# An opening rearranged: an early table request, row factors one product ahead, and copies and sine arguments moved from VectorE to ScalarE

## The chip, the cores and the metric

The kernel runs on one core of a Trainium2 chip. A core has five engines that run side by side, each in the order of its own list of instructions: TensorE (PE in the profile; its weight loads are shown apart as PEld), VectorE (DVE), ScalarE (ACT), GpSimd (POOL) and SyncE (SP). Instructions of one engine wait for those of another, and for data transfers (DMA), by semaphores. Transfers are issued here almost all by SP, a few by ACT. The metric is the device time of one execution in microseconds (us), as the median of several runs.

## The reference

The kernel computes one layer of a bidirectional encoder on 2048 positions of 1024 channels (fp32). Cut to what the opening touches, and with the rest named in a line each, the reference does this:

```
u = rms_norm(h)                      # row factor rsqrt(mean(h*h) + eps), then a gain per channel
P = u @ W_in                         # one combined projection, columns partitioned
# Hyena group: width-3 convolution of v, x1, x2, then z <- x1 * (h1 * z + d1 z); z <- x2 * (h2 * z + d2 z)
#   the filters h1, h2 come from a small sine network over position features:
hid  = sin(fr1 * (feat @ w1 + b1))
hid  = sin(fr2 * (hid @ w2 + b2))
filt = (hid @ w3) * decay window;    spectrum = rfft(filt)
# mLSTM group: width-3 convolution, chunkwise scan in both directions, output gate
# group norms, output projection, residual; cross-attention into mem, residual; squared-ReLU MLP, residual; final norm
```

What matters is that the row factor of the norm is one number per position, so that the projection can be made of the unscaled rows (times the gain) and multiplied by the row factor afterwards; and that the argument of each sine is a sum and a product, `fr * (v + b)`, which is the same as `fr * v + b * fr`.

## The kernel before, in words

Every fp32 matmul is made of three in a reduced type: an operand is split into a high part (a cast by ACT, L365) and a low part (the difference, by DVE, L365), and `mm3` issues high by high (L354), low by high (L357) and high by low (L358). A *product* of the input projection is 128 output columns by 512 positions: eight slices k of the channels, three matmuls each, 24 in all, into one of four banks of the accumulator called `mm`. A second set of four banks, `hy`, takes the small matmuls.

The projection's method `sweep` makes the products in order and counts them in `self.made`. Positions come in chunks of 512. For the first chunks, `x_first` loads the transposed rows x (tiles `xt`, and `a` for the second chunk), makes the operands `xh` (ACT, L557) and `xl` (DVE, L558), squares them on ACT (L563), adds the squares up on DVE (L565), sums over the channels with four one-column matmuls (`columns`, L570), takes the inverse root (L459 and the lines of `rsqrt`), spreads the result on a diagonal `dg` (DVE, L493), and makes of it with one matmul and an ACT copy the tile `rowb` of row factors (`rows`, L579 and L580). The drains of the products, `leave`, multiply each product by `rowb` on the way out of its bank (DVE, L752). They are held back in a list: up to three finished products may wait in their banks while a fourth is made.

Where these steps are placed among the matmuls is given by a table of hooks, keyed by (products made, slice k):

```
self.hooks = {(0, 5): second, (1, 5): lambda: operands(range(4)), (2, 1): lambda: columns(0), (2, 2): halfway,
              (3, 1): lambda: rows(0), (5, 1): lambda: columns(1), (5, 6): lambda: rows(1), (6, 0): third}
```

The written order is not the final one. A scheduler orders each engine's instructions by its own estimate of times; `keep_in_program_order` (pinning) holds an instruction at its written place against that, and `behind` holds a matmul only behind the matmul that was written before it. In the kernel before, the first of the four one-column matmuls and the matmul of `rows` are held by `behind`.

Into the projection is woven `filters`, which makes the Hyena filters: a matmul of the features (L275), a sine, a second matmul (L278), a sine, and from the hidden layer the filter blocks in groups (matmuls L177, L190; DVE L330 to L335; POOL L336; an ACT copy L314 and a store). One sine over 128 by 512 is six DVE instructions and the ACT function: `u = (v + b) * fr` (L250), the nearest multiple of two pi (L253, L254), its subtraction in two steps (L257, L258), a clamp (L259), and Sin on ACT (L260). There are eight sines. Behind a product, when its convolution is done (ACT L762, DVE L764, L765), `sweep_out` transposes it on PE (L791), and the helper `copy` brings the transposed tiles from the bank to a staging tile `st`, turn by turn on ACT (L205) and on DVE (L207), whence SP stores them.

Later chunks are loaded by `x_chunk` (loads L518 on SP, row factors L503, product with gain and factor on DVE L507, splits L365). Far behind the opening, the mLSTM scan (L1215 to L1320) is interleaved by the scheduler with the output projection, which belongs to another part of the program and has no line of the change in it.

Of the kernel before, what the change touches and what calls it, by code (L numbers as in the profile page):

```python
# [133 lines left out]
class Prog:  # L134
    def __init__(self, ctx, tc, a):
        self.tc, self.nc, self.a = tc, tc.nc, a
        nc = self.nc
        self.ctx = ctx
        self.dr = ctx.enter_context(tc.tile_pool(name="dr", bufs=1, space=DRAM))
        self.s = {}  # L140
        cp = self.cp = ctx.enter_context(tc.tile_pool(name="cp", bufs=1))
        ident = cp.tile([128, 128], F32, name="ident")
        nc.gpsimd.memset(ident, 1.0)
        nc.gpsimd.affine_select(ident, ident, pattern=[[-1, 128]], compare_op=ALU.is_equal, fill=0.0,
                                base=0, channel_multiplier=1)
        self.ident = ident
        self.eps = cp.tile([128, 1], F32, name="eps")
        nc.vector.memset(self.eps, EPS)
        self.ones = cp.tile([128, 128], F32, name="ones")
        nc.vector.memset(self.ones, 1.0)  # L150
        self.flip = 0
        self.banks = []
        self.pending = []
        self.prepq = None
        self.hooks, self.made, self.lag, self.rowb = {}, 0, [], None
        self.rbp = cp.tile([128, 16], F32, name="rbp")
        cp.tile([128, 8], F32, name="even")
        par = self.par = cp.tile([128, 192], F32, name="par")
        nc.scalar.dma_start(out=par, in_=a["par"])
        self.g_mix, self.g_mem, self.gx, self.gf = (par[:, 8 * i:8 * i + 8] for i in range(4))  # L160
        self.cw = par[:, 32:92].rearrange("p (i c) -> p i c", i=3)
        self.cb, self.gb = par[:, 92:112], par[:, 112:128]
        self.ps = ctx.enter_context(tc.tile_pool(name="ps", bufs=1, space=PSUM))
# [37 lines left out]

    def copy(self, out, in_):
        self.flip ^= 1
        if self.flip:
            self.nc.scalar.copy(out, in_)  # L205
        else:
            self.nc.vector.tensor_copy(out, in_)  # L207
# [28 lines left out]
    def filters(self):  # L236
# [3 lines left out]
        if True:  # L240
            fw = sb.tile([128, 1280], F32, name="fw")
            nc.sync.dma_start(out=fw, in_=a["fw"])
            w1, w2, w3 = fw[0:66, 0:128], fw[:, 128:256], fw[:, 256:1280].rearrange("p (o c) -> p o c", o=2)
            par = self.par[:, 128:132]
            f1 = sb.tile([128, 128], F32, name="f1")
            nc.sync.dma_start(out=f1, in_=a["c_f1"])

            def sine(dst, src, b, fr, first=False):
                u, k = tb(), tb()
                d = nc.vector.tensor_scalar(u, src, par[:, b:b + 1], par[:, fr:fr + 1], ALU.add, ALU.mult)  # L250
                if first:
                    tc.keep_in_program_order(d)
                nc.vector.tensor_scalar(k, u, 1.0 / TWO_PI, MAGIC, ALU.mult, ALU.add)  # L253
                nc.vector.tensor_scalar(k, k, -MAGIC, None, ALU.add)  # L254
                c1 = 6.28125
                c2 = TWO_PI - c1
                nc.vector.scalar_tensor_tensor(u, k, -c1, u, ALU.mult, ALU.add)  # L257
                nc.vector.scalar_tensor_tensor(u, k, -c2, u, ALU.mult, ALU.add)  # L258
                nc.vector.tensor_scalar(u, u, -PI_F, PI_F, ALU.max, ALU.min)  # L259
                nc.scalar.activation(dst, u if len(dst.shape) == 2 else u.rearrange("p (m g j) -> p m g j", g=2, j=16), AF.Sin)  # L260
# [270 lines left out]
    def x_first(self):  # L531
# [35 lines left out]
        def columns(c):  # L567
            p = self.hy()
            for t in range(4):
                d = nc.tensor.matmul(p[:, t:t + 1], ssum[c][:, 128 * t:128 * t + 128], self.ones[:, 0:1], start=True, stop=True)  # L570
                if t == 0:
                    self.behind(d)
            rx = self.rx[:, 4 * c:4 * c + 4]
            self.inv_rms(rx, p[:, 0:4])
            self.dg = self.diagonal(rx)

        def rows(c):
            p = self.hy()
            self.behind(nc.tensor.matmul(p, self.ones, self.dg, start=True, stop=True))  # L579
            nc.scalar.copy(self.rowb[c], p)  # L580
# [18 lines left out]
        def operands(ks):  # L599
            for k in ks:  # L600
                operand(x1, 1, k)
# [5 lines left out]
        def third():  # L607
            w2 = self.weights(sb, *self.items[2], kc=2, nbufs=4)
            self.wst = self.stream(sb, self.items[3:], w2, kc=2, nbufs=4)

        self.hooks = {(0, 5): second, (1, 5): lambda: operands(range(4)), (2, 1): lambda: columns(0), (2, 2): halfway,
                      (3, 1): lambda: rows(0), (5, 1): lambda: columns(1), (5, 6): lambda: rows(1), (6, 0): third}
        for _ in range(9):
            yield
        for c in (2, 3):
# [98 lines left out]
    def sweep(self, cols, hf, first, after=None):  # L714
# [3 lines left out]
        for run in [cols[:2]] + [[c2] for c2 in cols[2:]] if self.made == 0 else [[c2] for c2 in cols]:  # L718
# [7 lines left out]
            for c, c2 in [(c, c2) for c in range(2) for c2 in run]:  # L726
                wh, wl = ws[c2]
                for m in range(2):
# [5 lines left out]
                    for k in range(8):  # L734
                        if (self.made, k) in self.hooks:
                            self.hooks.pop((self.made, k))()
                        self.mm3(p, wh[:, k, ms], wl[:, k, ms], xh[:, k, cs], xl[:, k, cs], k == 0, k == 7,
                                 k == 0 and 3 < self.made < 13)

                    def leave(c=c, m=m, c2=c2, p=p, cc=cc, Ps=Ps, run=run):  # L740
                        if c == 0:
# [1362 lines left out]
```

## Time and profile before

| | us |
|---|---|
| three runs | 3126.70, 3130.87, 3132.18 |
| their median | 3130.87 |
| the profiled execution's own time | 3127.22 |
| its span, first to last instruction | 3125.4 |
| PE busy in the span | 3031.2 (97%) |
| DVE busy | 1960.3 (63%) |
| ACT busy | 1487.1 (48%) |
| POOL busy | 1146.5 (37%) |

The profile is that of one execution. Its rows give an engine, a source line, an operation, the tiles written and read, the busy time, and in brackets the idle time of the engine ahead of it with what released it. A matmul that runs behind another overlaps its tail, so the distance between two starts says more than the printed length. The column PEclk of a stretch is the clock granted to TensorE as a share of full speed; its mean over the run is 0.987. The time between the span and the execution's own time is 1.8 us.

### The profile page before, as it was taken

The page shows a single profiled execution, that of the slowest core. Times are in us where ns is not written, and L with a number is a line of the kernel's source. Part 1 is how long each engine was busy: PE and PEld are TensorE (multiplying, and loading weights), DVE is VectorE, ACT ScalarE, POOL GpSimd, SP SyncE. Part 2 cuts the span into 40 slices and gives each one's busy share as a digit, 9 for nine tenths or more (in the row PEclk, how much of TensorE's full clock was granted, in tenths as well). Part 3 has the DMA queues.
Part 4 walks back from the last instruction along what each step waited for, and adds up shares of the span by engine and source line. Part 5 has one row for each costly group of instructions (what it writes and reads, how often), then busy time and mean ns, then how long its engine had stood idle before and what let it go on. Part 6 is the DMA issues. An engine that isn't in the chain of part 4 may idle for free.

```text
span 3125.4 us, 42916 instructions
## 1 busy us (share of the span) xinstructions
PE 3031.2 (97%) x14257; PEld 2377.4 (76%) x14257; DVE 1960.3 (63%) x3448; ACT 1487.1 (48%) x2907; POOL 1146.5 (37%) x802
## 2 busy tenths in 40 slices
PE   8999999989999898999999999999999999999998
PEld 6655667766677666888888888888888888888876
DVE  7965466446646455777765556557555686565695
ACT  5443366533656225555544455556555443333335
POOL 0122012200113343324141327776565475242693
PEclk9999999999999998999999999999999999999999
DMA  6564767676877897455385647656644565353524
GB/s 211 153 212 163 235 204 220 192 217 217 240 207 246 267 315 242 142 184 197 115 280 175 226 154 246 207 187 219 213 151 150 167 216 187 111 165 112 161 91 172
DMA packets 444101, 607.07 MB, mean 194 GB/s; under 512 B 38494, under 2 KB 248542, under 8 KB 442856
## 3 DMA queue, kind: packets, MB, share of 16 engines
q1 hardware_dynamic: 405988, 546.54, 54.5%
q10 hardware_dynamic: 37892, 57.79, 5.4%
q8 instruction: 113, 1.85, 0.2%
q14 instruction: 108, 0.88, 0.1%
HBM read 401.79 MB, written 202.41 MB: 193 GB/s over the span
## 4 chain that ended last, share of the span: by engine, by line
PE 84%; DMA 6%; DVE 4%; ACT 2%; issue 2%; POOL 1%; SPq 0%; ACTq 0%; DVEq 0%; POOLq 0%
PE mm L354 17%; PE mm L358 17%; PE mm L357 17%; PE hy L358 6%; PE hy L354 6%; PE hy L357 6%; PE hy L177 3%; PE mm L912 2%; PE hy L943 2%; PE hy L985 1%; DMA a<-hy 1%; PE hy L1279 1%; PE mm L674 1%; PE mm L703 1%; PE hy L1281 1%
## 5 line engine op out<-in xcount | busy, mean ns | idle before, releaser
L1623 DVE TENSOR_TENSOR bl<-wr,bh 128x512 fp32r<-128x512 f32 x213 | 240.3, 1134 | 129.9 <-ACT bh L1622 129.7
L1622 ACT CAST ah<-w 128x512 fp32r<-128x512 f32 x284 | 176.6, 623 | 301.5 <-PE hy L357 155.2
L365 DVE TENSOR_TENSOR wl<-wn,wh 128x512 fp32r<-128x512 f32 (+1 forms) x300 | 218.1, 773 | 99.9 <-ACT wh L365 99.4
L354 PE MATMUL mm<-xh,wh 128*128 128x512 f32 x640 | 267.5, 419 | 12.1 <-ACT wh L365 9.1
L990 POOL TENSOR_TENSOR b<-b,a 128x512 f32<-128x512 f32 x64 | 87.4, 1367 | 509.3 <-ACT b L988 214.5
L357 PE MATMUL mm<-xl,wh 128*128 128x512 f32 x640 | 255.6, 399 | 0.7 <-DVE xl L365 0.6
L358 PE MATMUL mm<-xh,wl 128*128 128x512 f32 x640 | 254.8, 399 | 0.0
L1622 ACT CAST bh<-wr 128x512 fp32r<-128x512 f32 x232 | 143.5, 621 | 229.1 <-PE mm L358 177.0
L1623 DVE TENSOR_TENSOR al<-w,ah 128x512 fp32r<-128x512 f32 x236 | 216.7, 918 | 55.4 <-ACT ah L1622 55.2
L358 PE MATMUL mm<-bh,al 128*128 128x512 f32 x576 | 224.0, 391 | 2.6 <-POOL al L1623 2.6
L354 PE MATMUL mm<-bh,ah 128*128 128x512 f32 x576 | 225.9, 392 | 0.4 <-DVE acc L1785 0.3
L357 PE MATMUL mm<-bl,ah 128*128 128x512 f32 x576 | 224.9, 390 | 0.0
L365 ACT CAST wh<-wn 128x512 fp32r<-128x512 f32 (+1 forms) x300 | 166.6, 618 | 113.8 <-PE mm L358 51.4
L357 PE MATMUL mm<-act,wh 128*128 128x512 f32 x512 | 200.5, 393 | 0.8 <-DVE act L365 0.8
L354 PE MATMUL mm<-act,wh 128*128 128x512 f32 x512 | 198.8, 394 | 2.5 <-ACT wh L365 2.4
L358 PE MATMUL mm<-act,wl 128*128 128x512 f32 x512 | 199.1, 392 | 0.0
L354 PE MATMUL hy<-bh,ah 128*128 128x512 f32 x448 | 175.2, 391 | 0.0
L357 PE MATMUL hy<-bl,ah 128*128 128x512 f32 x448 | 174.6, 390 | 0.0
L358 PE MATMUL hy<-bh,al 128*128 128x512 f32 x448 | 174.4, 390 | 0.0
L354 PEld LDWEIGHTS mm<-xh,wh 128*128 128x128 f32 x640 | 121.3, 190 | 67.2 <-issue 19.0
L354 PE MATMUL mm<-wh,xh 128*128 128x256 f32 (+1 forms) x512 | 155.9, 305 | 10.6 <-ACT xh L365 8.1
L336 POOL TENSOR_TENSOR b<-b 128x512 f32<-128x512 f32 x32 | 58.3, 1822 | 277.4 <-DVE b L333 137.6
(369 smaller groups left out, 8282.3 us busy)
## 6 DMA issues: line engine op xcount, KB each, us to landing
wr<-hc SPq DMA_DIRECT2D x224, 256.0 KB
w<-in_ff_w_dram SPq DMA_DIRECT2D x172, 256.0 KB
hc<-wn SPq DMA_DIRECT2D x128, 256.0 KB
wn<-in_w_in_dram SPq DMA_DIRECT2D x100, 256.0 KB
hc<-q SPq DMA_DIRECT2D x96, 256.0 KB
fs<-a SPq DMA_DIRECT2D x32, 512.0 KB
a<-fs SPq DMA_DIRECT2D x64, 256.0 KB
a<-zs SPq DMA_DIRECT2D x64, 256.0 KB
```

The lines of the kernel that those rows point to most:

```text
L177: b = self.nc.tensor.matmul(*products[-1], start=True, stop=True)
L336: nc.gpsimd.tensor_tensor(e[1], f, b, ALU.subtract)
L354: first = mm(ps, lh, rh, start=start, stop=False)
L357: mm(ps, lh, rl, start=False, stop=False)
L358: self.last = mm(ps, ll, rh, start=False, stop=stop)
L365: both = (self.nc.scalar.copy(hi, src), self.nc.vector.tensor_tensor(lo, src, hi.bitcast(F32), ALU.subtract))
L674: mul(p[:, m], w[:, k, ms], mt[k // 4][:, k % 4], start=k == 0, stop=k == 7)
L912: nc.tensor.matmul(pp, dm[:, m], t[:, m], start=True, stop=True)
L943: nc.tensor.matmul(pg, em[:, m], y, start=True, stop=True)
L990: nc.gpsimd.tensor_tensor(xt, xt, hi[:, m], ALU.mult)
L1622: self.nc.scalar.copy(hi, src)
L1623: eng.tensor_tensor(lo, src, hi.bitcast(F32), ALU.subtract)
```

## The change

Four things change. First, a small tile that held nothing becomes `fb`, and ACT's first instruction is a one-column copy of a constant into it, which needs no transfer; ACT's function table is thus asked for by that copy. Second, `copy` uses ACT for all of its copies as long as fewer than 28 products are made, in place of every other one; 14 copies change from DVE to ACT. Third, the argument of a sine is made on ACT as `fr * v + fb`, with `fb = b * fr` multiplied once on DVE for each of the two layers; the eight instructions of L250 leave DVE, and eight activations appear on ACT. The instruction pinned in a sine is now DVE's next one. Fourth, the hooks of the first chunk's `columns`, `halfway` and `rows` move from slices 1, 2 and 1 to slices 5, 6 and 5; the first one-column matmul of the first chunk is pinned in place of being held behind, and so is the first matmul of each slice with a hook in products 2 and 3.

```diff
-        cp.tile([128, 8], F32, name="even")
+        self.fb = cp.tile([128, 8], F32, name="fb")
+        nc.scalar.activation(self.fb[:, 4:5], self.eps, AF.Copy)
...
     def copy(self, out, in_):
         self.flip ^= 1
-        if self.flip:
+        if self.flip or self.made < 28:
             self.nc.scalar.copy(out, in_)
...
+            for i in (0, 2):
+                nc.vector.tensor_tensor(self.fb[:, i:i + 1], par[:, i:i + 1], par[:, i + 1:i + 2], ALU.mult)
...
                 u, k = tb(), tb()
-                d = nc.vector.tensor_scalar(u, src, par[:, b:b + 1], par[:, fr:fr + 1], ALU.add, ALU.mult)
+                nc.scalar.activation(u, src, AF.Identity, bias=self.fb[:, b:b + 1], scale=par[:, fr:fr + 1])
+                d = nc.vector.tensor_scalar(k, u, 1.0 / TWO_PI, MAGIC, ALU.mult, ALU.add)
                 if first:
                     tc.keep_in_program_order(d)
-                nc.vector.tensor_scalar(k, u, 1.0 / TWO_PI, MAGIC, ALU.mult, ALU.add)
...
-                if t == 0:
+                if t == 0 and c == 0:
+                    pin(d)
+                elif t == 0:
                     self.behind(d)
...
-        self.hooks = {(0, 5): second, (1, 5): lambda: operands(range(4)), (2, 1): lambda: columns(0), (2, 2): halfway,
-                      (3, 1): lambda: rows(0), (5, 1): lambda: columns(1), (5, 6): lambda: rows(1), (6, 0): third}
+        self.hooks = {(0, 5): second, (1, 5): lambda: operands(range(4)), (2, 5): lambda: columns(0), (2, 6): halfway,
+                      (3, 5): lambda: rows(0), (5, 1): lambda: columns(1), (5, 6): lambda: rows(1), (6, 0): third}
...
                         if (self.made, k) in self.hooks:
                             self.hooks.pop((self.made, k))()
+                            hook = True
+                        else:
+                            hook = False
                         self.mm3(p, wh[:, k, ms], wl[:, k, ms], xh[:, k, cs], xl[:, k, cs], k == 0, k == 7,
-                                 k == 0 and 3 < self.made < 13)
+                                 k == 0 and 3 < self.made < 13 or hook and self.made in (2, 3))
```

Lines below the first edit carry higher numbers in the changed kernel (L354 becomes L357, L570 becomes L573, L579 becomes L584, L752 becomes L760).

What the scheduler makes of it shows at three places. The first is PE at the end of the first four products: `hy` from `dg` and `ones` is the matmul of `rows`, `mm_328`, `mm_249` and `mm_329` are products, `mm_384` and `mm_387` the one after, and the matmul from `fw` is the filters' first. Between the one-column matmuls and the end of the four products, 18 matmuls stand in both programs. Before:

```order
L570 MATMUL hy_252<-ones_65,ssum0_98 128x1 x4
...
L354 MATMUL mm_328<-xh_87,wh_106 128x512
L357 MATMUL mm_328<-xl_88,wh_106 128x512
L358 MATMUL mm_328<-xh_87,wl_107 128x512
L579 MATMUL hy_332<-dg_272,ones_65 128x512
L275 MATMUL hy_370<-b_366,fw_361 128x512
L354 MATMUL mm_384<-xh_87,wh_104 128x512
```

And with the change:

```order
L573 MATMUL hy_265<-ones_65,ssum0_99 128x1 x4
...
L361 MATMUL mm_249<-xh_88,wl_108 128x512
L584 MATMUL hy_345<-dg_285,ones_65 128x512
L357 MATMUL mm_329<-xh_88,wh_107 128x512
...
L361 MATMUL mm_329<-xh_88,wl_108 128x512
L278 MATMUL hy_373<-b_369,fw_362 128x512
L357 MATMUL mm_387<-xh_88,wh_105 128x512
```

The one-column matmuls stay where they were; the matmul of `rows` now follows them by 9 matmuls in place of 18, and the other 9 follow it.

The second place is DVE at about 115 us of the span before, around the drain of a product of the second chunk and the third chunk's first operands (`xt`, `xl`); rows from `hy` and `a`, and `b` from `b`, are the filter blocks. Before:

```order
L207 COPY st<-mm 126x512
L233 SCALAR_TENSOR_TENSOR xr_y<-xr_t,xr_y 128x2
L460 COPY small<-xr_y 128x2
L752 TENSOR_TENSOR P<-mm,rowb_101 128x512
...
L764 SCALAR_TENSOR_TENSOR cv<-P,par,cv 128x1008
L507 SCALAR_TENSOR_TENSOR xt<-xt,par,rb 128x512 x4
L330 TENSOR_TENSOR b<-hy,a 128x512
L331 TENSOR_TENSOR b<-hy,a 128x512
L765 SCALAR_TENSOR_TENSOR cv<-P,par,cv 128x1008
L365 TENSOR_TENSOR xl<-xt,xh 128x2x512
```

With the change:

```order
L333 TENSOR_TENSOR b<-hy,a 128x512
L334 TENSOR_TENSOR b<-hy,a 128x512
L336 TENSOR_TENSOR b<-b 1x512
L338 TENSOR_TENSOR b<-b 128x512
...
L760 TENSOR_TENSOR P<-mm,rowb_102 128x512
...
L772 SCALAR_TENSOR_TENSOR cv<-P,par,cv 128x1008
L510 SCALAR_TENSOR_TENSOR xt<-xt,par,rb 128x512 x4
L773 SCALAR_TENSOR_TENSOR cv<-P,par,cv 128x1008
L333 TENSOR_TENSOR b<-hy,a 128x512
```

Two groups of filter blocks, seven DVE rows, now stand ahead of that drain; before, they stood between it and the rows of the next operands and behind them. On PE their matmuls stand some 25 matmuls earlier. The copy of `st` is gone from DVE here.

The third place is DVE at about 1257 us before, where the mLSTM scan (`rw`, `ht`) meets the output projection (`act`). Before:

```order
L365 TENSOR_TENSOR act<-hy,act 128x4x128
L220 SCALAR_TENSOR_TENSOR hy<-hy,bry 128x8
L1251 TENSOR_TENSOR rw<-rw,hy 128x512 x2
L1313 SCALAR_TENSOR_TENSOR ht<-ht,hy,gml 128x128 x8
L1448 TENSOR_TENSOR acc<-mm,acc 128x512
```

With the change:

```order
L368 TENSOR_TENSOR act<-hy,act 128x4x128
L1321 SCALAR_TENSOR_TENSOR ht<-ht,hy,gml 128x128 x8
L368 TENSOR_TENSOR act<-hy,act 128x4x128
L1259 TENSOR_TENSOR rw<-rw,hy 128x512 x2
L1240 STREAM_SHUFFLE rw<-rows_9565 128x512 x2
```

The two rows on `rw` now stand behind the eight on `ht` and a row of `act`, which they led. PE's counterpart is that the matmuls from `rw` (L1279, L1281) stand together behind four of the projection's. No line of the change is there; the order follows from the scheduler's estimate of all that lies ahead.

## The prediction, made before the result was known

> **What bounds the kernel now.** I read the page's shares first, then PE's waits in the first 300 us, then a table of stretches, then the timeline at each place that the change touches. The page and the table of waits:
>
> ```profile
> PE 3031.2 (97%) x14257; PEld 2377.4 (76%) x14257; DVE 1960.3 (63%) x3448; ACT 1487.1 (48%) x2907; POOL 1146.5 (37%) x802
> ...
> PE mm L354 <- ACT wh L365: 9.1, 1, 9.1
> PE hy L579 <- DVE dg L493: 3.0, 1, 3.0
> PE hy L190 <- DVE b L335: 1.1, 1, 1.1
> ...
> PE hy L177 <- issue: 0.2, 1, 0.2
> ```
>
> PE is busy for 97% of the span, so nothing that the change does to DVE or ACT counts unless PE waits for them. In the first 300 us PE waits in eleven rows only: 9.1 us for the first weights, 3.0 us for the diagonal of the row factors, and nine rows that add up to 6.5 us (only the first and last of these nine are shown). Stretches of that time show what PE got done:
>
> ```profile
> core 0: us, PE busy (x) PEld busy (x) DVE busy (x) ACT busy (x) POOL busy (x), PEclk, DMA share, GB/s
> 34.40:37.80 3.40, 0.42 (x1) 0.30 (x2) 2.61 (x13) 0.00 (x0) 0.00 (x0) 1.00 0.00 0
> 37.80:44.60 6.80, 6.80 (x14) 3.97 (x13) 4.75 (x8) 1.87 (x2) 0.00 (x0) 0.50 0.00 0
> 57.00:117.00 60.00, 59.05 (x276) 47.77 (x275) 54.03 (x132) 29.48 (x56) 0.00 (x0) 1.00 0.64 191
> 120.00:157.30 37.30, 31.79 (x133) 18.31 (x132) 37.29 (x58) 14.88 (x22) 8.15 (x4) 1.00 0.45 141
> 157.30:160.70 3.40, 3.40 (x14) 1.52 (x12) 2.10 (x4) 0.37 (x1) 1.75 (x1) 0.50 0.94 306
> 160.70:180.00 19.30, 19.22 (x86) 11.23 (x83) 14.11 (x21) 10.52 (x16) 4.48 (x2) 1.00 0.63 222
> 200.00:240.00 40.00, 40.00 (x193) 23.77 (x192) 21.98 (x33) 14.70 (x25) 10.96 (x7) 1.00 0.54 186
> ```
>
> The reader is to see three things. From 120 to 157.3 us DVE is busy for 37.29 of 37.30 us, ACT for 14.88, and PE makes 133 matmuls; at the rate of the undisturbed stretch (193 in 40 us) they would take 27.6. So DVE bounds that stretch, and 9.7 us are lost in it, more than the waits there that the profile names. Ahead of it, from 57 to 117 us, DVE is busy for 90% and PE hardly waits. And the granted clock is 0.50 in two stretches: for 6.8 us behind the wait for the diagonal, and for 3.4 us at the end of the DVE-bound stretch.
>
> **The change part by part.** *The early table request.* ACT's table load starts when the first x tile lands, because the first activation needs both:
>
> ```profile
> 5.87 1.28 ACT L557 ACT_TABLE_LOAD   x1 [5.87 <-DMA xt<-in_x_t_dram]
> 7.16 1.33 ACT L557 ACTIVATE xh<-xt,par 128x512 fp32r<-128x512 f32 x2
> 8.40 1.12 ACT L365 CAST wh<-a 128x512 fp32r<-128x512 f32 x2
> 9.06 0.80 PE L354 MATMUL mm<-xh,wh 128*128 128x512 f32 x1 [9.06 <-ACT wh L365]
> ...
> 29.14 0.95 PE L570 MATMUL hy<-ones,ssum 128*128 128x1 f32 x8
> 30.12 0.16 DVE L459 TENSOR_SCALAR ms<-hy 128x4 f32<-128x4 f32 x1 [0.98 <-PE hy L570]
> ```
>
> With the table loaded beforehand, the first activation starts at 5.87, 1.28 us sooner, and the casts and PE's start follow if the weights and the next x tiles are there. ACT worked without a gap from 7.16 to 9.06, which shows no tile missing then; whether all later ones lead by as much isn't shown. Bounds: +0.5 (the later tiles come when they come, and half of it is lost) to +1.28. I take +1.2, since ACT's rows show no wait there. The DVE chain behind the one-column matmuls moves along. The new copy of one column lies in time in which ACT only waits for a transfer: 0.
>
> *Row factors one product ahead.* The one-column matmuls stay in place among PE's rows, and so does the DVE chain between them and the diagonal (with the six or seven additions of the second chunk's squares in it). The matmul that uses the diagonal stands 9 matmuls nearer:
>
> ```profile
> 33.26 0.39 PE L358 MATMUL mm<-xh,wl 128*128 128x512 f32 x1
> 33.49 0.39 PE L354 MATMUL mm<-xh,wh 128*128 128x512 f32 x1
> ...
> 34.59 0.69 DVE L565 TENSOR_TENSOR ssum<-ssum,sq 128x512 f32<-128x512 f32 x1
> 36.45 0.87 DVE L493 TENSOR_SCALAR dg<-ident,small 128x128 f32<-128x128 f32 x4
> 37.38 1.69 PE L579 MATMUL hy<-dg,ones 128*128 128x512 f32 x2 [3.05 <-DVE dg L493]
> ...
> 39.72 2.48 DVE L752 TENSOR_TENSOR P<-mm,rowb 128x512 f32<-128x512 f32 x4 [2.40 <-ACT rowb L580]
> ```
>
> Two matmuls stand 0.23 us apart, so PE arrives 9 x 0.227 = 2.0 us sooner and waits 3.05 + 2.0 = 5.1 us instead of 3.05; the 9 matmuls are made afterwards. That is -2.0. The wait brings a clock drop of 6.8 us at 0.5 already, worth 3.4 us; a longer wait can bring one stretch of 3.4 us more (-1.7) or, since the idle stretch ends at another place of the clock's steps, one less (+1.7). Bounds -3.7 to -0.3, taken -2.0, the row with no change in the number of steps. For the drains at 39.72 nothing is won: they wait for the same diagonal. The pins alone move no row of PE beyond these.
>
> *Copies and sine arguments off DVE.* Their rows between 40 and 160 us:
>
> ```profile
> L250 DVE TENSOR_SCALAR b<-hy,par 128x512 f32<-128x512 f32 x8 | 6.4, 802 | 0.0
> L207 DVE COPY st<-mm 126x512 f32<-126x512 f32 x8 | 5.5, 681 | 2.6 <-DMA hy<-st 2.6
> L205 ACT COPY st<-mm 126x512 f32<-126x512 f32 x8 | 4.7, 583 | 6.4 <-PE mm L791 6.4
> ```
>
> DVE loses 6.4 + 5.5 = 11.9 us of work there, and the 2.6 us in which it waited for a store to free a staging tile; the other six of the 14 copies come later, where PE is full (19.22 of 19.30 us behind 160.7), and count nothing. ACT gains as much in rows of some 0.6 us in stretches where it is busy for 49% and 40%. How much reaches PE? In the DVE-bound stretch at most the 9.7 us of the count, with the low-clock stretch behind it 9.7 + 1.7 = 11.4; at least half of the nine named waits, 3.2. DVE's 11.9 us exceed the 9.7, so it should cease to be the bound; I take 10.0, near the count. Late next are ACT's casts of the third and fourth chunk's operands, which stand behind copies now:
>
> ```profile
> 138.88 0.73 PE L354 MATMUL mm<-xh,wh 128*128 128x512 f32 x2 [0.97 <-ACT xh L365]
> 152.75 1.05 ACT L365 CAST xh<-xt 128x1024 fp32r<-128x1024 f32 x1 [9.91 <-DVE xt L507]
> 154.33 0.51 PE L354 MATMUL mm<-xh,wh 128*128 128x512 f32 x1 [1.02 <-ACT st L205]
> ```
>
> The wait for such a cast costs 0.97 us now, and the second one has a slack of its own of 9.91 us on ACT, all DVE's; I let one such wait come back, -1.0. Net +9.0. The added wait: DVE now waits for ACT at the head of each sine, and behind it drains and splits are queued; L250 has 0.0 idle ahead of it in all eight, so its matmul was done long before DVE came, which leaves ACT time. The two one-column multiplications into `fb` take less than 0.2 us each (L459's row of 0.16 is the nearest) and lie before the first operands: 0. The compiled program asks for tables 12 times, as before, so the new Identity and Copy rows cost no table load.
>
> *The order at 1257 us.* The two rows on `rw`, for which PE's next four matmuls wait, go behind eight rows on `ht` and one on `act`:
>
> ```profile
> 1258.39 0.69 DVE L365 TENSOR_TENSOR act<-hy,act 128x512 fp32r<-128x512 f32 x1 [0.40 <-ACT act L365]
> 1259.55 1.28 DVE L1251 TENSOR_TENSOR rw<-rw,hy 128x512 f32<-128x512 f32 x2 [0.39 <-PE hy L1241]
> 1260.43 0.38 PE L1279 MATMUL hy<-va,rw 128*128 128x129 f32 x2
> 1260.76 2.22 DVE L1313 SCALAR_TENSOR_TENSOR ht<-ht,hy,gml 128x128 f32<-128x128 f32 x8
> ```
>
> They are 2.22 us later; four matmuls that PE makes meanwhile cover some 0.4. I take -1.8, with 0 (PE has more of the projection ready) and -3.5 (a low-clock stretch behind it, 1.7) as ends.
>
> **The sum.** +1.2 - 2.0 + 9.0 - 1.8 = +6.4 us: the profiled execution's 3127.2 becomes 3120.8. That execution lies 3.7 us under the median of the three runs; set off from the median, 3130.87 - 6.4 = 3124.5.
>
> One rule speaks against a part of this. The row: the second low-clock stretch, from 157.3, follows waits of 1.02, 0.46 and 0.64 us, none of them long. The Trainium skill, "TensorE: Matmul & The Clock Gate", section "Why this matters for your kernels", asks for no idle gap above about 3 us between bursts and says that one window of idleness drops the clock. With the first drop, behind 3.05 us, the trace agrees; the second came without such a gap, so the trace differs. By the rule it would have another cause than DVE's lateness and stay: 1.7 us less in the sum. I go by the rows, in which it ends a stretch that DVE bounds.
>
> A second one bears on the copies. The same copy takes 583 ns on ACT and 681 on DVE in the rows above. The Trainium skill, "ScalarE: Activation LUTs", section "Rules for kernel authors", would have adds and multiplies on VectorE rather than ScalarE. By it the eight sine arguments would stay, and the relief be 5.5 us instead of 11.9; the trace, where an ACT row of that size takes no longer than DVE's, doesn't bear it out.
>
> **The rivals.** (a) *Same: relief by the named waits only.* DVE's stretch is held in part by its own inputs, the x transfers of the later chunks, and the low clock at 157.3 stays:
>
> ```profile
> 143.67 4.08 SPq L518 DMA_DIRECT2D xt<-in_x_t_dram  x2
> 164.24 2.74 DVE L507 SCALAR_TENSOR_TENSOR xt<-xt,par,rb 128x512 f32<-128x512 f32 x4 [4.74 <-DMA xt<-in_x_t_dram]
> ```
>
> SP spends 4.08 us on two issues, and DVE waits 4.74 us for such a tile a little later. Against it: DVE has no idle time ahead of that in the stretch. Then the relief is half of 9.7 less the 1.0 that comes back, 3.9: 1.2 - 2.0 + 3.9 - 1.8 = +1.3, so 3129.6. The rule on the clock leads to nearly the same side: 6.4 - 1.7 = +4.7, 3126.2.
>
> (b) *Slower: ACT's queue.* All copies of that time stand on ACT, and a copy that waits for a store holds up every cast behind it. DVE paid 2.57 us for one such wait:
>
> ```profile
> 93.69 0.69 DVE L207 COPY st<-mm 126x512 f32<-126x512 f32 x1 [2.57 <-DMA hy<-st]
> ```
>
> Two such waits ahead of the first cast of each of the two chunks make 2 x 2 x 2.57 = 10.3 us, against which stands DVE's whole relief of 10.0; with the other terms it is 10.0 - 10.3 - 1.0 + 1.2 - 2.0 - 1.8 = -3.9, and with three at each chunk -9.0, 3139.9. It decides from the point at which casts are late by 13.7 us in all (3.7 beyond the relief, which with -2.6 of the other terms makes 6.3). Against it: ACT has some 52 us of idle time in the two stretches together, and only one copy of the sixteen waited.
>
> (c) *The early parts do nothing,* because x tiles and weights bound the start: 1.2 less, +5.2, 3125.7, which lies with (a).
>
> **How the numbers follow.** 0.2%, 6.3 us, is about what a measurement of this kernel can tell from no change. My sum lies just on it. Forecast, a gain of 6.3 us or more: 0.50. Within 6.3 us: 0.36, of it (a) 0.16, the clock's rule 0.10 and (c) 0.10. Slower by over 6.3 us, (b): 0.14. The lower end takes the best bounds, 1.28 - 0.3 + 11.4 = 12.4, from the fastest run, 3126.7 - 12.4 = 3114. The upper end: the worst of (a), 0.5 - 3.7 + 3.2 - 1.0 - 3.5 = -4.5, gives 3135.4; I round to 3135 and leave out (b) in its larger forms.
>
> **What the profile afterwards would show.** The first matmul at about 7.9 us, the load of the table before 5 us; the wait for the diagonal at 5 us, with a low-clock stretch of 6.8 us behind it; DVE below 90% in the stretch at 120 to 150 us and its 133 matmuls in about 28 us, no low clock behind it; a wait of PE for `rw` of about 2 us near 1250. I am wrong if the casts on ACT wait behind copies, if the named waits for `xh` and `xl` grow, or if transfers of x set the pace there.

## The result, and the profile after

| | before | changed |
|---|---|---|
| median, us | 3129.22 (3126.70 to 3132.18, 6 runs) | 3119.57 (3116.15 to 3121.71, 6 runs) |
| ratio | 1 | 0.9971, 95% interval 0.9961 to 0.9980 |
| profiled execution: own time, span | 3127.22, 3125.4 | 3121.71, 3120.0 |

The change makes the kernel 9.1 us faster by the ratio; 6.4 us were forecast, in a range that held the time. A later set of runs of the same two kernels (among the experiments below) gave 3125.36 against 3127.11, ratio 0.9990 (0.9981 to 0.9999), which is 3.1 us: the gain has the same sign both times, and its size is known no better than between these two. Over both sets, 17 runs of the changed kernel average 3121.6 and 35 of the kernel before 3127.4, a gap of 5.8 us.

The table of PE's waits in the first 300 us of the changed kernel, to be held against the eleven rows of before:

```profile
PE mm L357 <- ACT wh L368: 8.0, 1, 8.0
PE hy L584 <- DVE dg L496: 4.7, 1, 4.7
PE hy L191 <- DVE b L338: 1.3, 1, 1.3
PE mm L360 <- DVE xl L368: 1.3, 1, 1.3
PE hy L178 <- POOL b L339: 1.0, 1, 1.0
```

The first wait is 1.1 us shorter, the second 1.7 us longer, and of the nine others, 6.5 us together, three are left with 3.6 us. The stretches of the prediction, in the changed kernel (us, then busy time of PE, PEld, DVE, ACT and POOL with their counts, granted clock, DMA share, GB/s):

```profile
33.56:40.39 6.83, 4.37 (x8) 2.85 (x9) 3.77 (x14) 0.59 (x1) 0.00 (x0) 0.50 0.00 0
...
57.00:117.00 60.00, 60.00 (x280) 47.57 (x279) 50.77 (x125) 36.16 (x68) 3.19 (x2) 1.00 0.64 202
120.00:157.30 37.30, 35.03 (x163) 20.79 (x159) 34.32 (x54) 18.07 (x28) 6.89 (x4) 1.00 0.66 219
157.30:160.70 3.40, 2.06 (x8) 0.59 (x10) 2.49 (x4) 1.04 (x1) 0.00 (x0) 1.00 0.18 67
160.70:180.00 19.30, 19.23 (x88) 11.42 (x84) 18.01 (x23) 10.89 (x18) 4.99 (x3) 1.00 0.67 233
```

From 120 to 157.3 us PE makes 163 matmuls in place of 133, DVE is busy for 34.32 us in place of 37.29, and the low clock at the end of that stretch is gone. The start of the opening, and the wait for the diagonal:

```profile
1.29 1.28 ACT L158 ACT_TABLE_LOAD   x1 [1.29 <-PEq L2087]
...
5.95 1.33 ACT L560 ACTIVATE xh<-xt,par 128x512 fp32r<-128x512 f32 x2 [3.16 <-DMA xt<-in_x_t_dram]
7.33 1.14 ACT L368 CAST wh<-a 128x512 fp32r<-128x512 f32 x2
8.00 0.80 PE L357 MATMUL mm<-xh,wh 128*128 128x512 f32 x1 [8.00 <-ACT wh L368]
...
35.09 0.88 DVE L496 TENSOR_SCALAR dg<-ident,small 128x128 f32<-128x128 f32 x4
36.02 2.08 PE L584 MATMUL hy<-dg,ones 128*128 128x512 f32 x2 [4.68 <-DVE dg L496]
```

The table load lies at 1.29 us, where ACT has nothing else to do, and the first matmul comes at 8.00 in place of 9.06.

Waits alone don't show where the time went, so I counted PE's matmuls and took, for the Nth of them, how much earlier it starts in a kernel than in the trace of before. This is worked out from the traces, row by row; both traces have 14257 matmuls, and the few that change places within a stage blur a point by a microsecond or two, so that only points between stages are used.

```
Nth matmul                 80   140   320   450  1000  3000  4000  5200  6000 14256
its start before, us       29    49    90   119   246   648   872  1134  1309  3111
changed                   1.0   0.5   0.5   1.8   7.3   7.2   8.1   8.0   7.7   5.4
changed, second time      2.0   2.1   2.1   3.4   9.0   8.9   6.4   4.4   6.3   7.1
```

The table shows where time is won: 1 us at the start, a small loss or none at the row factors (between the 80th and the 140th), and 6.7 to 6.9 us between 90 and 246 us. Of the 2.0 us at the 80th matmul of the second trace, about 1 us is not the change's: the granted clock rises to full speed 2.9 us after the first matmul there, against 4.9 us in the trace of before and 5.1 us in the first trace of the changed kernel. From 246 to 648 us the lead stays to within 0.1 us. Behind 648 us the two executions of one program part by up to 3.6 us.

### The profile page after: what moved, and what is told of

It reads as the page before. It is cut to its first block, busy times and chain, and to the rows that moved or that the text cites. A ratio compares the mean times of both kernels' runs of the same rounds, so it can differ in the third digit from the quotient of the medians.

```text
span 3120.0 us, 42912 instructions
## 1 busy us (share of the span) xinstructions
PE 3025.7 (97%) x14257; PEld 2374.8 (76%) x14257; DVE 1957.9 (63%) x3428; ACT 1498.4 (48%) x2930; POOL 1145.9 (37%) x802
## 4 chain that ended last, share of the span: by engine, by line
PE 55%; DVE 2%; issue 1%; DMA 1%; ACT 0%; POOL 0%; SPq 0%; ACTq 0%; POOLq 0%; DVEq 0%
PE mm L357 12%; PE mm L360 12%; PE mm L361 12%; PE hy L361 6%; PE hy L357 6%; PE hy L360 6%; DVE bl L1631 1%; PE hy L1287 1%; PE hy L1289 1%; DVE acc L1923 0%; PE hy L1534 0%; DVE acc L1957 0%; PE hy L1423 0%; DMA e<-hg 0%; PE hy L1249 0%
## 5 line engine op out<-in xcount | busy, mean ns | idle before, releaser
L357 PE MATMUL mm<-xh,wh 128*128 128x512 f32 x640 | 267.5, 419 | 8.6 <-ACT wh L368 8.0
L357 PE MATMUL mm<-bh,ah 128*128 128x512 f32 x576 | 225.6, 392 | 0.1
L357 PE MATMUL mm<-act,wh 128*128 128x512 f32 x512 | 198.9, 394 | 1.4 <-ACT wh L368 1.3
L357 PE MATMUL hy<-bh,ah 128*128 128x512 f32 x448 | 175.2, 391 | 0.0
L357 PEld LDWEIGHTS mm<-xh,wh 128*128 128x128 f32 x640 | 121.2, 190 | 60.9 <-issue 18.6
L357 PE MATMUL mm<-wh,xh 128*128 128x256 f32 (+1 forms) x512 | 155.2, 304 | 12.6 <-ACT xh L368 10.2
L361 PEld LDWEIGHTS mm<-xh,wl 128*128 128x128 f32 x640 | 121.0, 189 | 47.9 <-issue 23.2
```

Source lines behind the costliest of these rows:

```text
L357: first = mm(ps, lh, rh, start=start, stop=False)
L361: self.last = mm(ps, ll, rh, start=False, stop=stop)
```

## The experiments

All are compared with the kernel before. The line numbers of each kernel differ a little, as its edits do.

**The early table request alone.**

```diff
-        cp.tile([128, 8], F32, name="even")
+        self.fb = cp.tile([128, 8], F32, name="fb")
+        nc.scalar.activation(self.fb[:, 4:5], self.eps, AF.Copy)
```

> The kernel before with the early table request alone. Theory: the first matmul starts at about 8.0 us in place of 9.06, and the 1.0 us is kept, since the one-column matmuls and the diagonal move along: 1.0 us faster at the end of the first 100 us, and about 1 us faster in all (3128), with 1.5 us either way from rows that the scheduler orders otherwise. Rival: the x tiles and weights take the 1.0 us back within the first four products, and nothing is left when the one-column matmuls start (29.1 us before).

Measured 3128.27, ratio 0.9995 (0.9985 to 1.0004). PE's lead is 1.1 us at the 80th and the 320th matmul, so it is not taken back in the opening. Of that 0.8 us is left at 246 us: PE's rows up to there stand in the order of before, and its wait for a sine near 97 us is 1.4 us in place of 1.0. Nothing is left at the end of its trace (-2.0). 1 us is below what the timed runs tell apart, and they show no difference. The theory holds in the trace only; the rival falls.

**The row factors' hooks and pins alone.**

```diff
-        self.hooks = {..., (2, 1): lambda: columns(0), (2, 2): halfway,
-                      (3, 1): lambda: rows(0), ...}
+        self.hooks = {..., (2, 5): lambda: columns(0), (2, 6): halfway,
+                      (3, 5): lambda: rows(0), ...}
...
-                if t == 0:
+                if t == 0 and c == 0:
+                    pin(d)
+                elif t == 0:
                     self.behind(d)
```

(with the pins of the matmuls at the hooks, as in the change).

> The kernel before with the row factors' hooks and pins alone. Theory: the wait for the diagonal grows from 3.05 to about 5 us, and between 0.4 and 2.0 us are lost there, more when the low clock falls on matmuls and less when it falls on the wait; nothing is won later: 3129.6 to 3131.2. Rival: drains that start 9 matmuls sooner spare PE waits for banks further on, and the kernel gets faster by 2 us or more (3127 or less).

Measured 3127.71, ratio 0.9995 (0.9985 to 1.0006). The wait is what the theory said:

```profile
PE hy L581 <- DVE dg L493: 5.1, 1, 5.1
```

but only 0.2 us are lost between the 80th and the 140th matmul, since the low clock lasts 3.4 us there and partly falls on the wait. At 246 us this kernel leads by 3.0 us: the order behind is another, and no low-clock stretch ends the DVE-bound stretch:

```profile
120.00:157.30 37.30, 33.49 (x152) 20.37 (x150) 37.29 (x60) 15.57 (x22) 8.97 (x5) 1.00 0.55 167
```

DVE is as full here as before (37.29 us), and PE makes 152 matmuls in place of 133. So a part of such a count, 2.6 us between the 320th and the 1000th matmul, can come without any work taken off DVE. Both theories miss: no loss, and no gain that the runs show.

**The change without the row factors' part,** measured twice (the second time beside the changed kernel).

```diff
-        self.hooks = {..., (2, 5): lambda: columns(0), (2, 6): halfway,
-                      (3, 5): lambda: rows(0), ...}
+        self.hooks = {..., (2, 1): lambda: columns(0), (2, 2): halfway,
+                      (3, 1): lambda: rows(0), ...}
```

(and without its pins).

> The changed kernel with the hooks and pins of before. Theory: the wait for the diagonal is back at about 3 us, and the kernel is 0.4 to 2.0 us faster than the changed one (3117.5 to 3119.2). Rival: the row factors' place carries part of the gain behind 120 us, and this is slower than the changed kernel by 2 us or more (3121.6 or more).

> The changed kernel with the hooks and pins of before, once more, beside the changed kernel on the same chip. Theory: 0 to 2 us faster than the changed kernel, since its trace is 1.2 us ahead at the 120th matmul. Rival: slower than it by 2 us or more.

> The changed kernel once more, as the measure for the other three on the same chip: 0.9961 to 0.9980 of the kernel before, as measured first.

Measured 3119.57, ratio 0.9970 (0.9959 to 0.9981), and 3120.05, 0.9979 (0.9970 to 0.9988); the changed kernel beside the second gave the 0.9990 (0.9981 to 0.9999) told above, which is outside what was expected of it. The wait is back at 2.6 us. PE's lead grows by 0.3 to 0.5 us between the 80th and the 140th matmul, where the changed kernel loses 0.5 or wins 0.1. So the row factors' place costs some 0.2 to 1.0 us, and carries little of the gain behind 90 us (between the 320th and the 1000th matmul 6.2 and 6.3 us are won without it, 6.7 and 6.9 with it). That is small enough that one pair of medians (3119.57 and 3119.57) shows none of it; the other pair, 5.3 us apart where 0 to 2 were expected, shows more than the traces account for.

**Copies and sine arguments together, and each alone.**

```diff
-        if self.flip:
+        if self.flip or self.made < 28:
             self.nc.scalar.copy(out, in_)
```

```diff
-                d = nc.vector.tensor_scalar(u, src, par[:, b:b + 1], par[:, fr:fr + 1], ALU.add, ALU.mult)
+                nc.scalar.activation(u, src, AF.Identity, bias=self.fb[:, b:b + 1], scale=par[:, fr:fr + 1])
```

> The kernel before with the copies and the sine arguments on ScalarE, without the early table and without the new hooks. Theory (VectorE bounds the stretch from 120 to 157 us): PE is no sooner at 100 us than before, and 6 to 8 us sooner at 190 us; 6 to 8 us faster in all (3121 to 3123). Rival (the gain behind 120 us comes of the other two parts, or of rows in another order): less than 3 us (3126 or more).

> The kernel before with the copies alone moved to ScalarE; VectorE loses 5.5 us of work before 160 us. Theory (VectorE is the bound there, so relief counts by its microseconds): PE is 4 to 6 us sooner at 190 us, 3 to 6 us faster in all. Rival (the sine arguments carry the relief, since they stand ahead of the drains): less than 2 us.

> The kernel before with the sine arguments alone moved to ScalarE; VectorE loses 6.4 us of work before 160 us. Theory: PE is 4 to 6 us sooner at 190 us, 3 to 6 us faster in all; together with the copies alone more than the 7 us of both at once, since PE's full rate caps the sum. Rival: less than 2 us, if the wait of VectorE for ScalarE at the head of each sine eats the relief.

Measured: together 3121.42, ratio 0.9979 (0.9969 to 0.9989); copies alone 3120.18, 0.9977 (0.9968 to 0.9987); sine arguments alone 3117.95, 0.9972 (0.9961 to 0.9983). PE's lead over before:

```
Nth matmul                 80   140   320   450  1000  3000
copies and sines          0.9   1.3   1.3   2.5   7.7   7.6
copies alone              0.1   0.1   0.1   0.6   5.6   6.3
sines alone              -0.1   0.3   0.3   1.6   8.8   8.7
```

Between the 320th and the 1000th matmul both together win 6.4 us, the copies alone 5.5, the sines alone 8.5. The parts don't add up: either one alone wins most of what both win, or more, as if the other found little left. At 100 us both together are 2.5 us ahead, where no lead was expected: 0.9 us of it stands at the 80th matmul, where nothing was moved yet, and 1.2 us come at 98 us, where PE's wait of 1.0 us for a sine is gone. Each part alone wins more than the 3 to 6 us expected of it, 7 and 9 by the ratios. Stretches of the copies alone, then of the sines alone:

```profile
120.00:157.30 37.30, 34.85 (x149) 20.00 (x148) 36.61 (x60) 18.48 (x28) 8.79 (x5) 0.95 0.55 182
```

```profile
120.00:157.30 37.30, 36.45 (x167) 20.92 (x165) 35.38 (x56) 17.48 (x27) 8.72 (x4) 1.00 0.67 217
```

With the sines alone PE makes 167 matmuls there, more than with the whole change (163). In the first 300 us, behind the diagonal, PE waits for 1.0 us with the sines alone and for 3.9 us with both (for DVE's filter blocks, for `xl` and for POOL). As far as these traces go, moving the copies is of no use once the sine arguments are moved; the timed runs (0.9972 and 0.9979) don't tell the two apart.

**The work put back.** The changed kernel, with DVE writing 14 of the copies a second time and passing over each sine argument twice more (a product with one).

```diff
             self.nc.scalar.copy(out, in_)
+            if not self.flip:
+                self.nc.vector.tensor_copy(out, in_)
...
                 nc.scalar.activation(u, src, AF.Identity, ...)
+                for _ in range(2):
+                    nc.vector.tensor_scalar(u, u, 1.0, 0.0, ALU.mult, ALU.add)
```

> The changed kernel with VectorE's work put back and nothing else: behind 14 of ScalarE's copies VectorE writes the same tile once more (0.68 us each), and each sine gets two more VectorE passes that multiply by one (0.42 us each, in place of the 0.80 us of before). Theory (relief by work): the gain from 100 to 190 us falls from 6.6 us to less than 2, and the kernel is within 3 us of the kernel before. Rival (the gain comes of the order of the filter blocks or of banks that ScalarE frees sooner): most of it stays, 3122 or less.

Measured 3128.11, ratio 1.0002 (0.9993 to 1.0011): the gain is gone from the timed runs. Its waits beside the two of the opening, and the stretch:

```profile
PE hy L285 <- ACT b L267: 1.7, 1, 1.7
PE mm L361 <- ACT xh L372: 1.7, 1, 1.7
PE mm L364 <- DVE xl L372: 0.7, 1, 0.7
```

```profile
57.00:117.00 60.00, 58.29 (x266) 46.80 (x265) 53.73 (x138) 36.19 (x66) 0.00 (x0) 0.97 0.60 181
120.00:157.30 37.30, 34.30 (x146) 19.93 (x145) 37.04 (x60) 17.50 (x26) 7.79 (x4) 1.00 0.52 164
```

DVE is full again from 120 us on, with 37.04 of 37.30 us, and PE is down to 146 matmuls. The wait of 1.7 us for a sine costs 3.6 us by the 320th matmul, with a low-clock stretch at 70.7 us behind it. At 246 us the lead is 1.7 us. Between the 320th and the 1000th matmul it still grows by 4.5 us, where less than 2 was expected: PE comes to the stretch 2.8 us late, and no low clock ends it. DVE's own rows show what became of the relief. The last two `xl` rows of the fourth chunk's operands start 5.4 and 6.6 us sooner than before in the changed kernel, 1.1 and 2.2 us sooner here, and 1.9 us with the hooks alone.

So the gain goes with the work taken off DVE: it is there with the sines or the copies moved, and not with the work put back. Banks that ACT frees sooner are not needed for it, since the sines alone move no copy. The order is not separated from it: of PE's first 1000 matmuls 118 find no partner in the changed kernel's order, more than the 92 between the changed kernel and before, since the scheduler, which goes by its own estimate of times, makes another order for a fuller DVE. The copies alone stand in an order that differs from both by 123 and 125, and win nearly as much; so the gain isn't tied to one order. How much of it comes straight from a lighter DVE, and how much from the order that the scheduler makes of that, no run shows.

**More work taken off DVE.** The change without the row factors' part, with the rounding of each sine on ACT too.

```diff
-                d = nc.vector.tensor_scalar(k, u, 1.0 / TWO_PI, MAGIC, ALU.mult, ALU.add)
...
-                nc.vector.tensor_scalar(k, k, -MAGIC, None, ALU.add)
+                nc.scalar.activation(k, u, AF.Identity, bias=self.fb[:, 5:6], scale=1.0 / TWO_PI)
+                nc.scalar.activation(k, k, AF.Identity, bias=self.fb[:, 6:7])
```

> The changed kernel with the hooks and pins of before, and two more steps of each sine (the rounding by adding and taking away a large constant) on ScalarE: VectorE loses 16 passes of 0.42 us, 6.7 us more. Theory (relief is capped by PE's full rate; 158 matmuls from 120 to 157 us there against 180 at full rate, so 22 x 0.207 = 4.6 us are left at most): 0 to 3 us faster than without it. Rival (ScalarE's longer way to the sine holds up the filter blocks and the drains behind them): slower than without it by 2 us or more.

Measured 3123.02, ratio 0.9985 (0.9976 to 0.9995), against 0.9970 and 0.9979 without it; 3.0 us slower than the latter on the same chip, though the two intervals overlap. Groups of rows from 40 to 160 us, and a wait of PE:

```profile
L257 ACT ACTIVATE b<-b,fb 128x512 f32<-128x512 f32 x8 | 5.8, 720 | 0.1
L256 ACT ACTIVATE b<-b,fb 128x512 f32<-128x512 f32 x8 | 5.7, 715 | 0.1
L260 DVE SCALAR_TENSOR_TENSOR b<-b 128x512 f32<-128x512 f32 x8 | 5.5, 689 | 5.1 <-ACT b L257 5.1
```

```profile
PE hy L283 <- ACT b L265: 1.7, 1, 1.7
```

A pass that took DVE some 0.42 us takes ACT 0.72, DVE idles 5.1 us for it at the head of its queue, and PE waits 1.7 us for a sine in a stretch where it had not waited; its lead falls by 2.2 us between the 140th and the 320th matmul, where it does not fall without the edit, and is 5.6 us at 246 us in place of 8.0 and 7.5. The trace and the medians speak for the rival: past the point at which DVE ceases to be the bound, the longer way through ACT costs.

**A filled gap.** The change without the row factors' part, with matmuls that nobody reads behind the one-column matmuls; measured twice.

```diff
             p = self.hy()
+            if c == 0:
+                for _ in range(12):
+                    pin(nc.tensor.matmul(p, self.xh[:, 0, 0:128], self.xh[:, 0, 0:512], start=True, stop=True))
...
```

(the matmul of `rows` is pinned behind them).

> The changed kernel with the hooks and pins of before, and 12 matmuls that nobody reads (2.7 us at 0.227) put behind the one-column matmuls, so that PE has no gap while VectorE makes the diagonal. Theory (the gap of about 3 us brings the low clock): no wait above 0.5 us there and no low-clock stretch before 60 us; 12 matmuls cost the 2.6 us that the wait cost, and the 3.4 us of the low clock are won: 3 us faster than without them, 3116.5. Rival (the low clock comes of something else, such as the one-column matmuls or the share of work in a longer time): the stretch at 0.5 stays, and the time is that without them, 3119.6, or 0.4 more.

> The kernel with 12 matmuls that nobody reads in the gap, once more, beside the one without them on the same chip. Its trace was 4.9 us ahead of the other's at 246 us and 1.8 us ahead at the end. Theory (the lead is real, and part of it is lost at about 1250 us, where the order differs): 1 to 4 us faster than without them. Rival (the lead is lost altogether): no faster than without them.

Measured 3119.84, ratio 0.9979 (0.9970 to 0.9988), and 3118.97, 0.9968 (0.9956 to 0.9980). PE's waits from 0 to 200 us, the first time:

```profile
PE mm L357 <- ACT wh L368: 7.9, 1, 7.9
PE mm L357 <- DVE P L760: 1.5, 1, 1.5
PE mm L360 <- DVE xl L368: 1.3, 1, 1.3
PE hy L178 <- POOL b L339: 1.1, 1, 1.1
```

The wait for the diagonal is gone, with 1.5 us for the first drain in its place, and from 20 to 130 us there is no low clock either time. The leads in the second expectation were taken without the 12 extra matmuls in the count; with them, the lead over the kernel without them is 1.3 and 2.6 us at the 140th matmul (the two times), 2.0 and 3.6 at 246 us. The row factors' place itself shows between the 80th and the 140th matmul: 2.2 us are won there both times, against 0.5 and 0.3 without the extra matmuls. The mechanism of the first expectation holds, then, but at 1.7 to 1.9 us and not at 3.4, since the wait of 1.5 us for the first drain takes the rest. The end doesn't show it: one median is 0.3 us above its pair, the other 1.1 us below, just inside the 1 to 4 expected. What becomes of the lead is told next.

**Where leads are lost.** Beyond 648 us, the lead of the same program differs from one execution to the next:

```
Nth matmul                       1000  3000  4000  5200  6000 14256
start before, us                  246   648   872  1134  1309  3111
without row factors               8.0   7.9   6.5   8.2   8.6   8.9
the same, second time             7.5   6.9   4.2   5.3   7.8   8.0
gap filled                       10.0   9.9  10.5   8.5   9.0   9.0
the same, second time            11.1  11.1   6.6   5.8   6.7   7.0
```

Between 648 and 872 us these four change by -1.4, -2.7, +0.6 and -4.5, and the changed kernel's two by +0.9 and -2.5. There the second half of x is loaded, and PE waits for it in all of them. A stretch of before, then a stretch of the gap filled (second time), and its two longest waits of PE from 640 to 700 us:

```profile
665.00:690.00 25.00, 16.95 (x88) 12.68 (x84) 12.04 (x18) 5.20 (x9) 0.00 (x0) 0.73 0.93 291
```

```profile
640.00:665.00 25.00, 16.10 (x98) 11.09 (x96) 9.97 (x17) 5.25 (x10) 0.00 (x0) 0.91 1.00 280
```

```profile
PE mm L357 <- ACT xh L368: 8.8, 2, 6.2
PE hy L178 <- DMA a<-zg: 3.0, 1, 3.0
```

The DMA engines are busy for 0.93 to 1.00 of the time there, and PE's waits, the longest of 5 to 10 us, bring low clocks of 10 to 17 us in all. A PE that arrives sooner finds the same transfers under way. That part of a lead is lost to them is what the shares suggest; no run changed those transfers, so it isn't shown.

## Why the prediction was right, point by point

- *The early table request,* forecast +1.2 within 0.5 to 1.28: the first matmul is 1.06 us earlier, and 1.0 us is left at the 80th. Right, and it kept. That later tiles lead by enough was the open point; they do.
- *Row factors,* forecast -2.0 within -3.7 to -0.3, with a wait of 5.1 us and 6.8 us of low clock. The wait was 4.7 (4.8 the second time), the low clock 6.8 (3.4 the second time), yet the term measured -0.5 and +0.1 (-0.2 with the hooks alone). The step that failed is the one that kept the low clock's price when its length stayed. The longer wait and the low clock share their time: in the stretch from 33.56 to 40.39 PE is busy for 4.37 us where it was busy for all of 6.80, so the low clock costs 4.37/2 = 2.2 us in place of 3.4, which gives back 1.2 of the 1.6 that the wait lost.
- *Copies and sine arguments,* forecast +9.0 (10.0 less 1.0 that comes back): 6.7 and 6.9 by the counts. The mechanism was right as far as the put-back work shows it (the gain goes with DVE's work); the term was mis-sized. The failed step is "I take 10.0, near the count". DVE is still busy for 34.32 of 37.30 us from 120 on, and PE makes 163 matmuls, not the 180 of full rate. DVE stayed at 92% there, where less than 90% was forecast. What is relieved early brings DVE's later rows forward: of its first 40 rows of filter blocks (`b` from `hy` and `a`) those that I compared, every fourth, start 7 to 17 us sooner than before, and from 160.7 to 180 us DVE is busy for 18.01 us where it was busy for 14.11. PE gets less of this than DVE does. That the scheduler's new order has a part in it isn't excluded, as said above. One wait came, but not the forecast one: the waits of 1.0 us for ACT's cast and copy are gone, and the wait for `xl` grew from 0.6 to 1.3 us, because DVE's product `xt` stands behind filter blocks and a convolution (ACT's cast waits 5.14 us for it). Growing waits for `xl` were named as a sign of being wrong; at 0.7 us it is a small one.
- *The added waits.* DVE's wait for ACT at the head of a sine was costed at nothing. Three groups of rows of the changed kernel from 40 to 160 us (busy time and mean ns; idle time ahead and what ended it):

```profile
L254 DVE TENSOR_SCALAR b<-b 128x512 f32<-128x512 f32 x8 | 3.4, 426 | 2.0 <-ACT b L253 2.0
L206 ACT COPY st<-mm 126x512 f32<-126x512 f32 x16 | 8.8, 585 | 6.6 <-PE mm L799 4.3 <-DMA hy<-st 2.3
L253 ACT ACTIVATE b<-hy,fb,par 128x512 f32<-128x512 f32 x8 | 6.1, 769 | 5.6 <-PE hy L278 5.6
```

DVE waits 2.0 us in all at L254, which reaches PE nowhere by name. ACT's copies wait 2.3 us for a store, as DVE's did (2.6), and PE has no wait for a cast of `xh` left in the first 300 us: rival (b) didn't come. (Its turning point of 13.7 us leaves out the 1.0 that comes back, which its sum counts; with it, 12.7.)
- *The order at 1257 us,* forecast -1.8: no wait of PE for `rw` appears in the changed kernel from 1195 to 1300 us, and the leads around the place (from the 5200th to the 6000th matmul) change by -0.3 and +1.9. The cost isn't seen; the end 0 of its range was right. The step that failed is that PE has only 0.4 us of cover: ahead of the matmuls from `rw` it has four of the projection, the transposes and the eight from `qn` in a stretch at low clock, and DVE's rows came in time.
- *The second low clock.* I went by the rows; it is gone in the changed kernel. The second time there was one of 3.4 us at 140.6 instead, behind other waits. The rule of the Trainium skill, "TensorE: Matmul & The Clock Gate", section "Why this matters for your kernels" (no idle gap above about 3 us), would have kept it; these traces differ from it, with the numbers in the last section. Whether such a stretch falls is in part chance: in the step ahead of the one of before PE was idle for 1.57 us, and by the table in the last section only 4 of 43 steps with 1.5 to 1.75 us were followed by a low clock. Up to 1.7 us of the leads at 246 us may thus be owed to the one execution of before that was traced.
- *The sum:* 1.0 - 0.5 + 6.7 = 7.2 at 246 us in one trace and 9.0 in the other, against 6.4 forecast. Two costs that were forecast too high, by about 1.8 us each, offset a gain that was forecast 2.2 us too high; that the sum came so near is in part luck. The sum of 7 to 9 fits the 9.1 of the first set; the 3.1 of the second lies below it, in the range of what is lost or not behind 648 us.

## What to carry to other kernels

In a stretch that one engine fills, taking work off it pays, but not by the microsecond: here 5.5 us of work off DVE won 5.5, 6.4 won 8.5, and both together 6.4. So try each part alone before keeping both. A pass moved to a less busy engine is worth it while it is off the way to what PE waits for; two more moved steps of a sine lost about 2 us of what the first had won. A wait that is lengthened where the clock drops anyway is cheaper than its length.

## What the runs showed of the hardware

*The low clock follows idle time summed over a step, not one gap.* The clock's changes in these traces lie on a grid of 3.413 us. Over 14 traces (the twelve experiments and the two kernels, 20 to 1300 us) I summed PE's idle time in each step at full clock and noted the clock of the next step:

```
idle in a step, us   next step full   next step at 0.5
under 1.25                4833                 0
1.25 to 1.5                 59                 1
1.5 to 1.75                 39                 4
1.75 to 2.0                  3                 9
2.0 and more                 0                80
```

About half a step of idleness, 1.7 us, decides in these traces, and it may be made of pieces: in 12 of the 94 steps ahead of a drop no single gap reaches 1.5 us. The step before the second low clock of the kernel before is such a one:

```profile
153.86:157.27 3.41, 1.84 (x6) 1.08 (x7) 3.41 (x5) 3.02 (x6) 0.00 (x0) 1.00 0.56 156
157.28:160.69 3.41, 3.41 (x14) 1.54 (x12) 2.12 (x4) 0.39 (x1) 1.75 (x1) 0.50 0.95 306
```

PE is busy for 1.84 of 3.41 us, idle for 1.57 in several waits, and the next step runs at half clock. The way back asks for a nearly full step: of 102 low steps with less than 0.5 us of idle time 91 were followed by full speed, of 120 with more only 3.

*One program, several times.* Where the grid falls against the program differs from one execution to the next (the first low clock begins at 33.56 us in one trace of the changed kernel and at 34.76 in the other), so the same gap costs one step or two or none. The 17 runs of the changed kernel, sorted by the mean granted clock that each recorded:

```
clock   runs   mean us
0.988     7    3123.9
0.989     3    3122.5
0.990     5    3119.3
0.991     2    3118.4
```

One step at half clock costs 1.7 us and 0.0005 of the mean clock, so 0.003 are about six steps and 10 us; the means differ by 5.5, in the same direction. Part of the spread from run to run thus goes with the clock, and a difference of 0.2% between two kernels lies within that spread.
